# The first two branch gates as one pair of seven products, queries and keys in their place, and values ahead of the x0 projections

## The chip, the cores and the metric

The kernel runs on one core of one Trainium2 chip. A core has TensorE (PE, matrix products into the accumulators of PSUM), VectorE (DVE), ScalarE (ACT), GpSimd (POOL) and SyncE (SP, which here does nothing but issue DMAs). The metric is the device time of one execution in microseconds (us); lower is better.

## The reference, cut to what matters

One layer of a hybrid backbone is computed for 128 context tokens and 512 latent tokens, 640 in all, with 1,024 channels in float32. The layer input is modulated (`h = x * (1 + scale) + shift`) and goes through one wide projection; everything else hangs on it:

```python
z = h @ w_in
hy, g_h, qkv, g_a, m = split(z)
v_h, x1, x0 = split(short_conv(hy))             # Hyena branch
q, k, v = split(qkv)                            # attention branch, 16 heads of 64
y_h = (fft_conv(v_h * x1, filters) + d * v_h * x1) * x0
y_a = attention(q, k, v)                        # context, or neighbourhood plus cached context
p_h = (y_h * silu(g_h)) @ w_bh
p_a = (y_a * silu(g_a)) @ w_ba
out = (sigmoid(m_h) * p_h + sigmoid(m_a) * p_a) @ w_out
y = layer_norm(alpha * x + gate * out)
```

The branch gates of the title are tiles of `g_a`; values are `v`; the x0 projections give `x0`. The keys and values of the context tokens are outputs too (`new_k`, `new_v`).

## The kernel before, in words

**Precision and tiles.** Channels lie on the 128 partitions, tokens along the free dimension. The modulated input is kept as a high and a low part (`hH`, `hL`, split by `split`, L101), eight blocks of 128 channels each; blocks 2 and 3 lie in tiles of their own (`hHp`, `hLp`). A weight tile is 1,024 input channels by 128 output channels and is split likewise into `wh` and `wl`. A product is three matmuls: high by high, high by low, low by high. A projection tile (`proj`, L188; `accumulate`, L178) is 8 blocks x 3 products x 2 halves of 320 tokens, into two of the four accumulator banks of `ps_mm`. With "dma" a weight's low part is made by a ScalarE negation (L162), an accumulating GpSimd DMA (L163) and a ScalarE copy for the high part (L164), with no VectorE work. There are two `raw`, two `wh` and three `wl` buffers.

**Pairs by seven products.** In the heads two weight tiles are computed together as a 2 x 2 block product (two halves of tokens, two tiles) with seven block products in place of eight (`pair_tile`, L1213). A block product is 4 blocks x 3 products, in matmuls of 320 tokens. Its operands are sums of token blocks, `t1` to `t4`, made in the first stage by `token_sums` and kept in DRAM (`tok_d`), and sums of weight blocks (`blocks`, `sum1`, `sum6`). The order of the products and of the operands they take is

```python
ORDER = ("b11", "t2", "t3", "t1", "b21", "t4", "b22")
```

`high` (ScalarE, L1191) and `low` (VectorE, L1199) make the weight parts four products ahead, and `post` combines the products on VectorE (L1221, L1226).

**First stage.** After a prologue (modulation, first tiles), a planner orders the instructions by their place in the program and by the times it expects. The program there is a weave of a main line and a side line, two steps of the first to three of the second. The main line runs over rounds q: `quarter_head(q + 1)` (two v_h and two x1 tiles, each with a short convolution on VectorE, L490), `quarter_tail(q)` (two x0 tiles, with convolutions too), and in the first two rounds `values(2 + q)`, which stores its result to DRAM; then `hand_over` with the last x0 tiles, values(1) and values(0), the first queries and keys, and the weights of the first two gate tiles. A convolution needs one of two `zs` buffers, into which ScalarE empties the accumulators (L482 to L486), and `u` or `x1` buffers (four and two of them). Values need two accumulator banks and, for the fifth block of tokens, a third; those stored to DRAM are copied through the two buffers that x1 also uses. The side line computes the filter spectra (L379 on) and the long convolution (L540 on) by matmuls and VectorE products.

**Heads.** From `first_gates` on, the order on all engines is written out by hand (`manual_schedule`), SyncE's DMAs included. First come the two gate tiles, with the first three weight parts of pair 0 between them; then `sums_of_second` (two accumulating loads for pair 1), `scratch` (four copies that put `hHp` and `hLp` into the second half of token rows 0 and 1 of `hH` and `hL`, and hand the freed tiles over as scratch), the loads of t1, of pair 1's block, of t4, and the first biases. `keys` (L856) loads the cached keys, and `k_half` stores the context keys with

```python
nc.sync.dma_start(o["new_kT"][j], kp)
```

A DMA on SyncE's queue waits there for what it reads; the DMAs behind it wait too. For each of eight heads `mains` (L1377) yields the steps of the pairs named in `HEADS`, and `attend` (L1112) gives the attention steps, which in head 0 come after fixed steps of the main line. The last stage, with the branch projections, output projection and layer norm, follows.

Of the kernel before, what the change touches and what calls it, by code (L numbers as in the profile page):

```python
# [10 lines left out]
F32 = mybir.dt.float32  # L11
# [9 lines left out]
NT = 640  # L21
# [11 lines left out]
T_Q, T_K, T_V, T_GA, T_MH, T_MA, T_BH, T_BA, T_WO = 32, 40, 48, 56, 64, 72, 80, 88, 96  # L33
# [13 lines left out]
def tile_hyena_natten_step(ctx: ExitStack, tc: tile.TileContext, a, o):  # L47
    nc = tc.nc
    P = 128
# [59 lines left out]
    out = {"x0": {}}  # L109
# [34 lines left out]
    early, raws, banks = {}, {}, {}  # L144

    def wraw(i):
        raws[i] = wp.tile([P, 1024], F32, tag="raw", name=f"raw{i}")
        load_to(raws[i][:], a["wall"][i])

    def wtile(i, eng=None, dst=None, width=P):  # L150
        if i in early:
            return early.pop(i)
        if i not in raws:
            wraw(i)
        if dst is None:
            wh = wp.tile([P, 1024], F32R, tag="wh", name=f"wh{i}")
            wl = wp.tile([P, 1024], F32R, tag="wl", bufs=3, name=f"wl{i}")
            dst = [wh[:]], [wl[:]]
        raw, n = raws.pop(i), 1024 // len(dst[0])
        if eng == "dma":  # L160
            (wh,), (wl,) = dst
            nc.scalar.activation(wl, raw[:], AF.Copy, scale=-1.0)  # L162
            nc.gpsimd.dma_start(wl, a["wall"][i], accum_op=ALU.add)  # L163
            nc.scalar.activation(wh, raw[:], AF.Copy)  # L164
        else:
            for j, (wh, wl) in enumerate(zip(*dst)):
                split(wh, wl, raw[:, n * j : n * j + n], eng)
        return [[w[c // n][:, c % n : c % n + width] for c in range(0, 1024, width)] for w in dst]
# [328 lines left out]
    def gate_tile(i, dst, eng=None):  # L497
        ps = yield from proj(i, eng=eng)
        for p, cs in zip(ps, CS):
            nc.scalar.activation(dst[:, cs], p[:, :HALF], AF.Tanh, scale=0.5)  # L500
            gate(dst[:, cs], p)

    def quarter_head(q):
        us = []
        out[f"u{q}"] = us
        for i in range(2):
            n = 2 * q + i
            u = hw.tile([P, NG + 1], F32, tag="u", bufs=4, name=f"u{n}")
            x1 = hwa.tile([P, NG + 1], F32, tag="cv", bufs=2, name=f"x1_{n}")
            yield from conv_tile(n, u)  # L510
            yield
            yield from conv_tile(8 + n, x1)
            nc.vector.tensor_tensor(u[:, :NG], u[:, :NG], x1[:, :NG], op=ALU.mult)
            us.append(u)
            yield
        out[f"whole{q}"] = True
# [10 lines left out]
    def quarter_tail(q):  # L527
        for i in range(2):
            n = 2 * q + i
            out["x0"][n] = row(yhp, "yh", f"x0_{n}", n=NG + 1)  # L530
            yield from conv_tile(16 + n, out["x0"][n])
            yield
        if q < 3:
            gate_convs(q)
# [121 lines left out]
    def values(m, home=None):  # L656
        w = [wtile(T_V + 2 * m + i, "dma", width=256) for i in range(2)]
        ps = [acc(f"v{m}_{i}") for i in range(2)]

        def passes(k):  # L660
            wh, wl = w[k // 4][0][k % 4], w[k // 4][1][k % 4]
            return ((hH, wh, k == 0, False), (hL, wh, False, False), (hH, wl, False, k == NK - 1))

        for half in range(2):
            ks = range(4 * half, 4 * half + 4)
            for k in ks:
                for x, wk, first, last in passes(k):
                    for t in range(4):
                        nc.tensor.matmul(  # L669
                            ps[t // 2][:, t % 2 * 256 : t % 2 * 256 + 256], x[:, k, P * t : P * t + P], wk,  # L670
                            start=first and t % 2 == 0, stop=last, skip_group_check=True,
                        )
                yield
            if half:
                parts = [ps[0][:], ps[1][:]]
            else:
                pe = acc(f"ve{m}")
            for k in ks:
                for x, wk, first, last in passes(k):
                    nc.tensor.matmul(pe[:, :256], x[:, k, P * 4 :], wk, start=first, stop=last, skip_group_check=True)  # L680
            yield
        if home is None:
            v = out[f"v{m}"] = slot(m, "v", f"v{m}")
            for c, p in ((0, parts[0]), (512, parts[1]), (1024, pe[:, :256])):
                nc.scalar.activation(v[:, c : c + p.shape[-1]], p, AF.Copy)
        else:
            for i, p in enumerate(parts):
                v = hwa.tile([P, NG + 1], F32, tag="cv", bufs=2, name=f"v{m}_{i}")
                nc.scalar.activation(v[:, :512], p, AF.Copy)
                nc.scalar.activation(v[:, 512:640], pe[:, 128 * i : 128 * i + 128], AF.Copy)  # L690
                nc.sync.dma_start(home[m][:, 512 * i : 512 * i + 512], v[:, :512])
                nc.sync.dma_start(home[m][:, 1024 + 128 * i : 1152 + 128 * i], v[:, 512:640])
                if i == 0:
                    nc.sync.dma_start(o["new_v"][:, m * 256 : m * 256 + 256], v[:, :256])
            yield
            return
        nc.sync.dma_start(o["new_v"][:, m * 256 : m * 256 + 256], v[:, :256])
        yield
# [61 lines left out]
    def chain(*gens):  # L760
        for g in gens:
            yield from g
# [58 lines left out]
    def queries(j):  # L821
        for hf, p in enumerate((yield from proj(T_Q + j, eng="dma"))):
            q_half(j, hf, p[:, :HALF])
        yield
# [31 lines left out]
    def keys(j):  # L856
        cached_keys(j)
        for hf, p in enumerate((yield from proj(T_K + j, eng="dma"))):
            k_half(j, hf, p[:, :HALF])
        yield  # L860

    def hand_over():
        yield from quarter_tail(3)
        load_sums(0, SUMS[:2])
        yield from values(1, v_d)
        hwa_stack.close()
        out["slots_l"] = left.enter_context(tc.tile_pool(name="slots_l", bufs=1, reuse_waits="tile"))
        out["slots_q"] = left.enter_context(tc.tile_pool(name="slots_q", bufs=1, reuse_waits="tile"))
        first_blocks()
        gate_convs(3)  # L870
        yield from chain(values(0), queries(0), keys(0))
        for i in range(2):
            wraw(T_GA + i)
        for i in range(2):
            early[T_GA + i] = wtile(T_GA + i, "dma")
        load_a(0)

    def first_gates():
        yield from gate_a(0)
        for g in range(AHEAD - 1):  # L880
            if g == 1:
                sum1(0)
            high(g)
            low(g)
        yield from gate_a(1)

    tail = ctx.enter_context(ExitStack())
    ac = ctx.enter_context(ExitStack())
# [26 lines left out]
    at = sp = tp = None  # L915
# [203 lines left out]

    N_ATT = 4  # L1120

    def gate_a(j):
        out[f"sg{j}"] = sg = at.tile([P, NT], F32, tag="sg", bufs=2, name=f"sg{j}")
        yield from gate_tile(T_GA + j, sg[:], "dma")
        yield


    def operand(name, p):
        if name in tok:
            return lambda i, k: tok[name][i][k // 2][:, HALF * (k % 2) : HALF * (k % 2) + HALF]  # L1130
# [173 lines left out]
        return pair_tile(p, use)  # L1304

    N_PAIR = 14
    HEADS = ("q1 h0 m0", "q2 h1 m1", "q3 m2 a2", "q4 h2 m3", "q5 m4 a4", "q6 h3 m5", "q7 a6", "m6 m7")
    MAKE = dict(a=gates_a, h=gates_h, q=queries_keys, m=mix)

    def tiles_of(item):  # L1310
# [12 lines left out]

    def quarters():
        for q in range(3):
            yield from chain(quarter_head(q + 1), quarter_tail(q))
            if q < 2:
                yield from values(2 + q, v_d)

    def convs():  # L1330
        yield from chain(until("whole0"), long_conv(0))
# [65 lines left out]

    engines = {getattr(mybir.EngineType, e) for e in ("PE", "DVE", "Activation", "Pool", "SP")}
    with tc.manual_schedule(engines=engines):
        for _ in first_gates():  # L1400
            pass
        sums_of_second()
        scratch()
        load_sums(0, SUMS[2:3])
        load_sums(1, SUMS[2:3])
        load_a(1)
        load_sums(0, SUMS[3:])
        load_sums(1, SUMS[3:])
        biases[0] = [bias_tile(h) for h in range(2)]
        for j in range(8):  # L1410
            side, n_main, n_side = attend(j), N_PAIR * len(HEADS[j].split()), N_ATT if j < 7 else N_ATT + 3
            done = taken = 0
            for _ in mains(j):
                done += 1
                while done in (14, 24, 36) if j == 0 else taken * n_main < done * n_side:
                    if next(side, StopIteration) is StopIteration:
                        break
                    taken += 1
                    if j == 0:
                        break  # L1420
            for _ in side:
                drain()
        drain()
# [311 lines left out]
```

## Time and profile before

| | us |
|---|---|
| median of 3 runs | 883.93 (883.04 to 885.12) |
| the profiled execution | 883.7 |
| its span, first to last instruction | 881.9 |
| TensorE busy | 866.0 (98%) |
| VectorE busy | 645.1 (73%) |
| ScalarE busy | 450.2 (51%) |
| GpSimd busy | 189.0 (21%) |

All times within the execution are counted from the start of the span. Stages: the prologue lasts to about 50 us, the first stage with the planner to about 344, the two gate tiles to 358, the heads to about 703, and the branch and output projections to the end. Matmuls are pipelined: the record of one is longer than the time to the next, so rates are read from counts in a stretch. "Granted clock" is the share of TensorE's full clock.

### The profile page before, as it was taken

The numbers are of one execution on the slowest core, as the hardware profiler recorded it, in microseconds if no ns is written. First come the engines' busy times: TensorE is split into PE (matmuls) and PEld (weight loads), VectorE is DVE, ScalarE is ACT, GpSimd is POOL, SyncE is SP. The second block draws the span as 40 slices with busy tenths as digits, with TensorE's granted clock in tenths as the row PEclk, the third lists the DMA queues.
The fourth block names the chain that finished last, engine by engine and source line by source line (L and its number), as shares of the span: only waits on it lengthen the run. The fifth ranks groups of instructions, "written<-read, shape, count | busy, mean of one in ns | idle before, by whom it ended". The sixth has DMA issues, their size and how long they took to land.

```text
span 881.9 us, 17167 instructions
## 1 busy us (share of the span) xinstructions
PE 866.0 (98%) x6464; PEld 836.8 (95%) x6464; DVE 645.1 (73%) x1229; ACT 450.2 (51%) x960; POOL 189.0 (21%) x216
## 2 busy tenths in 40 slices
PE   8999999989999999999999999999999999999996
PEld 7899999979999999999999999999999999999885
DVE  4778986596895852787867787677778488667666
ACT  4396555546446453566566556656666532243200
POOL 0012210100100112084353334333454200000000
PEclk9999999989999999999999999999999999999999
DMA  8978886435664799978776668675854587445521
GB/s 326 400 170 226 231 215 145 92 103 138 162 132 96 202 228 241 308 218 252 172 238 164 220 153 260 138 212 158 232 138 120 180 301 246 160 165 187 183 88 56
DMA packets 75822, 168.82 MB, mean 191 GB/s; under 512 B 11067, under 2 KB 29243, under 8 KB 75740
## 3 DMA queue, kind: packets, MB, share of 16 engines
q1 hardware_dynamic: 56492, 123.32, 41.9%
q0 software_dynamic: 13632, 38.80, 22.8%
q10 hardware_dynamic: 5616, 5.61, 1.9%
q8 instruction: 51, 0.84, 0.4%
q14 instruction: 31, 0.25, 0.1%
HBM read 143.06 MB, written 23.99 MB: 189 GB/s over the span
## 4 chain that ended last, share of the span: by engine, by line
PE 94%; DVE 3%; DMA 1%; ACT 1%; issue 1%; SPq 0%; POOL 0%; POOLq 0%; DVEq 0%; ACTq 0%
PE mm L183 33%; PE sp L1238 30%; PE out L1545 6%; PE v L669 5%; PE s L1044 2%; PE s L951 2%; PE pt L1035 2%; PE ve L680 1%; DMA t<-tok_d 1%; PE adaT L253 1%; PE adaT L270 1%; PE yb L171 1%; PE yb L173 1%; PE yb L172 1%; PE ut L547 1%
## 5 line engine op out<-in xcount | busy, mean ns | idle before, releaser
L1238 PE MATMUL sp<-t,wb 128*128 128x320 f32 x1056 | 166.3, 311 | 0.4 <-DMA t<-tok_d 0.4
L1238 PEld LDWEIGHTS sp<-t,wb 128*128 128x128 f32 x1056 | 157.1, 188 | 1.2 <-DMA t<-tok_d 0.6
L1238 PE MATMUL sp<-hH,wb 128*128 128x320 f32 x524 | 126.4, 312 | 0.0
L1238 PEld LDWEIGHTS sp<-hH,wb 128*128 128x128 f32 x524 | 90.0, 188 | 2.6 <-issue 2.6
L163 POOL DMA_DIRECT2D wl<-wall x32 | 28.4, 889 | 248.2 <-ACT wl L162 212.5
L1238 PE MATMUL sp<-hL,wb 128*128 128x320 f32 x262 | 81.0, 309 | 0.0
L183 PE MATMUL mm<-hH,wh 128*128 128x320 f32 x312 | 77.6, 315 | 0.9 <-ACT hH L329 0.6
L183 PE MATMUL mm<-hH,wl 128*128 128x320 f32 x312 | 75.0, 312 | 0.4 <-DVE wl L103 0.4
L183 PE MATMUL mm<-hL,wh 128*128 128x320 f32 x312 | 74.7, 311 | 0.0
L1199 DVE TENSOR_TENSOR wb<-s,wb 128x512 fp32r<-128x512 f32 x66 | 47.1, 715 | 23.3 <-ACT wb L1191 23.2
L164 ACT ACTIVATE wh<-raw 128x1024 fp32r<-128x1024 f32 x32 | 34.0, 1061 | 58.9 <-PE mm L183 49.5
L1191 ACT ACTIVATE wb<-s 128x512 fp32r<-128x512 f32 x66 | 41.6, 632 | 37.8 <-PE sp L1238 19.1
L1006 POOL TENSOR_SCALAR edge<-edge,sm 128x320 f32<-128x320 f32 x32 | 43.1, 1526 | 66.6 <-DVE sm L1004 66.6
L183 PEld LDWEIGHTS mm<-hH,wh 128*128 128x128 f32 x312 | 53.6, 190 | 2.9 <-ACT zs L485 0.9
L1006 POOL TENSOR_SCALAR p<-p,sm 128x384 f32<-128x384 f32 x32 | 50.9, 1675 | 25.3 <-PE sp L1238 11.4
L183 PEld LDWEIGHTS mm<-hH,wl 128*128 128x128 f32 x312 | 53.1, 189 | 1.2 <-DVE wl L103 0.9
L183 PEld LDWEIGHTS mm<-hL,wh 128*128 128x128 f32 x312 | 53.1, 189 | 0.7 <-DVE hL L330 0.5
L1238 PEld LDWEIGHTS sp<-hL,wb 128*128 128x128 f32 x262 | 49.3, 188 | 0.0
L1545 PE MATMUL out<-woh,yhs 128*128 128x512 f32 (+1 forms) x176 | 45.5, 372 | 0.0
L1226 DVE TENSOR_TENSOR spare_hHp<-sp,yu 128x320 f32<-128x320 f32 x66 | 32.0, 484 | 17.3 <-PE sp L1238 11.8
L183 PE MATMUL mm<-yhs,wh 128*128 128x320 f32 x224 | 42.5, 309 | 0.0
L102 ACT ACTIVATE wh<-raw 128x1024 fp32r<-128x1024 f32 x15 | 15.8, 1058 | 46.9 <-PE mm L183 38.7
(414 smaller groups left out, 2269.1 us busy)
## 6 DMA issues: line engine op xcount, KB each, us to landing
raw<-wall SPq DMA_DIRECT2D x52, 512.0 KB, 3.8
wl<-wall POOLq DMA_DIRECT2D x32, 512.0 KB, 6.7
ra<-wall SPq DMA_DIRECT2D x22, 512.0 KB, 4.2
rb<-wall SPq DMA_DIRECT2D x42, 256.0 KB, 5.1
ada<-wada SPq DMA_DIRECT2D x16, 512.0 KB, 8.2
tm<-bias SPq DMA_DIRECT2D x16, 512.0 KB, 8.6
s<-wall SPq DMA_DIRECT2D x22, 256.0 KB, 4.5
s<-wall POOLq DMA_DIRECT2D x22, 256.0 KB, 4.4
```

The costliest lines, as they stand in the source:

```text
L163: nc.gpsimd.dma_start(wl, a["wall"][i], accum_op=ALU.add)
L164: nc.scalar.activation(wh, raw[:], AF.Copy)
L183: nc.tensor.matmul(ps[hf][:, :HALF], wt[k], x[:, hf * HALF : (hf + 1) * HALF], start=(i == 0 and k == 0), stop=(i == lead[2] and k == NK - ...
L669: nc.tensor.matmul(ps[t // 2][:, t % 2 * 256 : t % 2 * 256 + 256], x[:, k, P * t : P * t + P], wk, start=first and t % 2 == 0, stop=last, ...
L951: nc.tensor.matmul(dst[h], x[rows(h), qs], y[rows(h), ks], start=i == 0, stop=i == 2, skip_group_check=True)
L1006: nc.gpsimd.tensor_scalar_mul(pv, pv, sm[:, 2, c : c + 1])
L1035: nc.tensor.transpose(pt[:, i * P : i * P + P], ps[h][:, c : c + P], ident)
L1191: nc.scalar.activation(made[g][:, 0], block(g), AF.Copy)
L1199: nc.vector.tensor_tensor(made[g][:, 1], block(g), f(made[g][:, 0]), op=ALU.subtract)
L1226: nc.vector.tensor_tensor(c, dst, c if j == 3 else ps["u"], op=ALU.add)
L1238: nc.tensor.matmul(dst, wk, x(xi, k), start=j < 4 and k == 0 and i == 0, stop=k == 3 and i == 2, skip_group_check=True,)
L1545: ins = nc.tensor.matmul(dst, m[k][:, c0 : c0 + P], w[:, c : c + n], start=(first and k == 0), stop=(last and k == 5), skip_group_check=True,)
```

## The change

Tiles 0 and 1 of the branch gates are no longer two single tiles ahead of the heads, but one more pair, `a0`, second in head 0. `first_gates` becomes `first_head`: the first queries and the first keys are computed where the gate tiles were, with the same three weight parts of pair 0 between them; `hand_over` ends after values(0) with the two weight tiles of queries and keys. The attention steps of head 0 come at main steps 14, 32 and 48 of 56 instead of 14, 24 and 36 of 42. In the rounds of the first stage the values are placed before the x0 projections (`quarter_tail`) instead of after them.

```diff
     gate_convs(3)
-    yield from chain(values(0), queries(0), keys(0))
-    for i in range(2):
-        wraw(T_GA + i)
-    for i in range(2):
-        early[T_GA + i] = wtile(T_GA + i, "dma")
+    yield from values(0)
+    for t in (T_Q, T_K):
+        wraw(t)
+    for t in (T_Q, T_K):
+        early[t] = wtile(t, "dma")
     load_a(0)
 
-def first_gates():
-    yield from gate_a(0)
+def first_head():
+    yield from queries(0)
     for g in range(AHEAD - 1):
         if g == 1:
             sum1(0)
         high(g)
         low(g)
-    yield from gate_a(1)
+    yield from keys(0)
...
-def gate_a(j):
-    out[f"sg{j}"] = sg = at.tile([P, NT], F32, tag="sg", bufs=2, name=f"sg{j}")
-    yield from gate_tile(T_GA + j, sg[:], "dma")
-    yield
...
-HEADS = ("q1 h0 m0", "q2 h1 m1", "q3 m2 a2", "q4 h2 m3", "q5 m4 a4", "q6 h3 m5", "q7 a6", "m6 m7")
+HEADS = ("q1 a0 h0 m0", "q2 h1 m1", "q3 m2 a2", "q4 h2 m3", "q5 m4 a4", "q6 h3 m5", "q7 a6", "m6 m7")
...
 def quarters():
     for q in range(3):
-        yield from chain(quarter_head(q + 1), quarter_tail(q))
+        yield from quarter_head(q + 1)
         if q < 2:
             yield from values(2 + q, v_d)
+        yield from quarter_tail(q)
...
-    for _ in first_gates():
+    for _ in first_head():
         pass
...
-            while done in (14, 24, 36) if j == 0 else taken * n_main < done * n_side:
+            while done in (14, 32, 48) if j == 0 else taken * n_main < done * n_side:
```

## The prediction

> **What bounds the kernel now.** I read the page first, then busy time by stretch, then the timelines of the two places where TensorE loses time, then SyncE's queue.
>
> ```profile
> span 881.9 us, 17167 instructions
> PE 866.0 (98%) x6464; PEld 836.8 (95%) x6464; DVE 645.1 (73%) x1229; ACT 450.2 (51%) x960; POOL 189.0 (21%) x216
> PEclk9999999989999999999999999999999999999999
> ```
>
> TensorE is busy for 98% of the span, so a gain is either fewer matmuls or less lost time, and what another engine gains counts only there. The columns of the next rows are the stretch, its length, each engine's busy time and count, the granted clock, DMA share and GB/s.
>
> ```profile
> 171.00:178.00 7.00, 7.00 (x49) 6.92 (x48) 7.00 (x12) 3.80 (x6) 1.43 (x2) 1.00 0.82 199
> 178.00:186.00 8.00, 3.71 (x17) 2.43 (x16) 8.00 (x8) 3.99 (x8) 1.47 (x2) 0.77 0.72 176
> 186.00:189.00 3.00, 3.00 (x12) 3.00 (x13) 3.00 (x5) 1.54 (x3) 0.00 (x0) 0.50 0.28 71
> 189.00:196.00 7.00, 7.00 (x51) 6.91 (x50) 7.00 (x12) 1.46 (x6) 0.00 (x0) 0.99 0.08 21
> 740.00:760.00 20.00, 20.00 (x138) 20.00 (x138) 14.75 (x17) 4.06 (x6) 0.00 (x0) 1.00 0.62 215
> ```
>
> The last row is undisturbed projection: 20.00 / 138 = 0.145 us for a matmul of 320 columns, in issue rate (the 0.31 us of a single record overlaps its neighbours). The first four show the one large loss of the first stage. Before and after it, 100 matmuls in 14 us are 7.14 a us; from 178 to 189 there are 29 in 11 us, where 78.6 would fit. That is 49.6 / 7.14 = 6.9 us lost, the part at clock 0.50 included. What TensorE waits for there:
>
> ```profile
> 180.22 0.39 PE L172 MATMUL fa<-sl,dftH 128*128 128x256 f32 x1 [0.99 <-DVE sl L103]
> 184.22 0.58 PE L171 MATMUL fb<-sh,dftH 128*128 128x256 f32 x1 [3.15 <-ACT sh L102]
> 185.80 0.63 PE L183 MATMUL mm<-hH,wh 128*128 128x320 f32 x1 [0.15 <-ACT zs L485]
> 180.03 2.87 DVE L591 TENSOR_TENSOR X<-X,F 128x2560 f32<-128x2560 f32 x1
> 184.16 0.93 DVE L490 SCALAR_TENSOR_TENSOR u<-zs,pack,u 128x641 f32<-128x641 f32 x1
> 185.19 0.28 ACT L482 ACTIVATE zs<-mm 128x128 f32<-128x128 f32 x1 [1.02 <-DVE u L490]
> ```
>
> The filter's matmuls (fa, fb) wait behind VectorE's spectral product and two convolutions. The next projection cannot fill the hole: its accumulators are held by an earlier projection until ScalarE empties them into zs at 185.19, and zs itself is released by VectorE's `u` at 184.16 + 0.93. By the program's order the tile at 171 to 178 is an x0 projection, and the one held up at 185.80 is the second.
>
> The other place is the first pair of the heads, from 358.49. These rows are TensorE's, ScalarE's and SyncE's:
>
> ```profile
> 358.49 0.31 PE L1238 MATMUL sp<-hH,wb 128*128 128x320 f32 x1
> 367.30 1.27 PE L1238 MATMUL sp<-t,wb 128*128 128x320 f32 x7
> 368.99 1.00 PE L1238 MATMUL sp<-t,wb 128*128 128x320 f32 x5 [0.41 <-DMA t<-tok_d]
> 345.34 0.54 ACT L839 ACTIVATE k<-mm 128x64 fp32r<-128x64 f32 x3
> 345.76 0.29 ACT L842 ACTIVATE kp<-mm 128x128 f32<-128x128 f32 x1
> 358.54 0.77 ACT L500 ACTIVATE sg<-mm 128x320 f32<-128x320 f32 x2 [1.91 <-PE mm L183]
> 346.07 0.34 SPq L843 DMA_DIRECT2D new_kT<-kp  x1
> 352.52 1.34 SPq L64 DMA_DIRECT2D hH<-hHp  x2
> 354.23 1.11 SPq L64 DMA_DIRECT2D hL<-hLp  x2
> 355.45 1.97 SPq L64 DMA_DIRECT2D t<-tok_d  x4
> 357.46 0.43 SPq L64 DMA_DIRECT2D ra<-wall  x1
> 357.99 2.65 SPq L64 DMA_DIRECT2D t<-tok_d  x4
> SPq L64 <- PE mm L183: 6.3, 2, 6.0
> SPq L843 <- ACT kp L842: 5.3, 2, 2.8
> ```
>
> The last two are SyncE's waits (total, times, longest). The token sums t1 and t4, eight loads, stand behind the four copies of hH and hL. These copies waited 6.0 us for the last gate tile's matmuls on token rows 0 and 1, which come first in that tile, so they left 6 us before the pair. Even so t4, the operand of the pair's sixth product, is late: seven matmuls from 367.30 take 7 x 0.145 = 1.0 us, to 368.31, and the next starts at 368.99, 0.7 us late. There is no slack to give away here.
>
> **The change part by part.** *Matmuls.* Two gate tiles are 2 x 8 blocks x 3 products x 2 halves = 96 matmuls; a pair by seven products is 7 x 4 x 3 = 84 of the same 320 columns. 12 x 0.145 = 1.7 us less. The added VectorE work (seven low parts, two sums, five combinations) is costed from
>
> ```profile
> L1199 DVE TENSOR_TENSOR wb<-s,wb 128x512 fp32r<-128x512 f32 x66 | 47.1, 715 | 23.3 <-ACT wb L1191 23.2
> L1226 DVE TENSOR_TENSOR spare_hHp<-sp,yu 128x320 f32<-128x320 f32 x66 | 32.0, 484 | 17.3 <-PE sp L1238 11.8
> ```
>
> as 9 x 0.72 + 5 x 0.48 = 8.9 us, beside 84 x 0.145 = 12.2 us of TensorE. The heads already run 22 such pairs this way, so I put it at nothing; without that cover it would be up to 8.9 us. The DMAs of the pair (512 + 5 x 256 = 1,792 KB) replace 4 x 512 = 2,048 KB and move later. The new steps 14, 32, 48 only spread the same attention steps over 56 steps instead of 42: nothing.
>
> *Queries and keys in first_head.* Their 96 matmuls stay in front of the first pair, so TensorE's work there is the same in another order. But the keys bring two DMAs into SyncE's written-out order, ahead of the copies: the load of the cached keys and the store of `kp`. SyncE holds everything behind that store until ScalarE has made `kp`, which is after the last matmul of the keys. ScalarE starts to empty a finished tile at 358.54, which is the pair's start; `kp` ends 345.76 + 0.29 - 345.34 = 0.71 us after the first copy of k, so it is ready 0.8 us after the pair's start. The store takes 0.34 us to issue, then four copies at about 0.49 (1.97 / 4, the issue rate of four loads in a row) take 2.0. The first t1 load leaves 3.1 us after the pair's start. Now it leaves at 355.45, 3.0 us before it: 6.1 us later. Queued behind are both t1 and t4, the second pair's raw block and the first biases; TensorE waits for t1 and t4. If they then arrive at the present pace, the lateness grows by the whole 6.1 us. Lower end: the present pace is partly slow.
>
> ```profile
> 355.00:363.00 8.00, 8.00 (x56) 8.00 (x56) 5.56 (x11) 4.55 (x9) 0.00 (x0) 1.00 0.89 287
> 363.00:369.00 6.00, 5.59 (x39) 5.28 (x37) 4.93 (x12) 2.79 (x8) 0.00 (x0) 1.00 1.04 408
> DMA to landing us min/median/max: 3.3/7.2/9.6
> ```
>
> The last row is the landing time of the sixteen sum loads. The first lands after 3.3 us at best; the 2,752 KB (2.82 MB) behind it at 408 GB/s take 6.9, together 10.2 us, against the 13.5 from 355.45 to 368.99. That would give back 3.3, leaving 2.8. Upper end: the second pair's two accumulating loads (512 KB) now fall into the same time, 0.52 MB / 408 = 1.3 more, 7.4. I take the middle of 2.8 and 6.1, **+4.5 us**. The keys' own finishing copies also wait for the cached keys, now loaded late; I cost that at nothing because the wait for t1 covers it, and it reaches TensorE only if t1 is early.
>
> *Values in front of x0.* In the second round, where the loss sits, TensorE would have values at 171 instead of an x0 projection. Values need no zs and nothing of VectorE:
>
> ```profile
> 299.76 0.64 PE L669 MATMUL v<-wh,hHp 128*128 128x256 f32 x4
> 300.24 0.64 PE L669 MATMUL v<-wh,hLp 128*128 128x256 f32 x4
> 198.58 0.87 DVE L513 TENSOR_TENSOR u<-u,x 128x641 f32<-128x641 f32 x1
> ```
>
> Four matmuls take 0.48 us, so the 96 that need only two accumulators take 11.5 us, where the x0 tile took 48 x 0.145 = 7.0: 4.5 us more filling than before, against 0.99 + 3.15 + 0.15 = 4.3 us of idle time. With the idle time the halved clock behind it would go too. The x0 convolutions then fall after VectorE's crowded stretch. Against it: the values' copies go into the two buffers of x1, of which the second is released only by the product at 198.58, so accumulators may stay held. The planner also rearranges this stage. The price is between a gain of 6.9 us (all of it) and a loss of 4.3 (one more such hole); I take **-5.5**, near the gain's end, because the filler is longer than the hole, and leave 1.4 for the held buffers. The first round has no hole and the sum takes nothing from it.
>
> *The sum*, against the profiled execution's own 883.7 us (its span is 881.9, the rest lies around it; the median shown is 883.93): 883.7 - 1.7 + 4.5 - 5.5 = **881.0 us**.
>
> **The rivals.** (a) *Slower.* The hole stays: the third accumulator is asked for before the second half of the values, so TensorE stands again until 185, and the sums come 6.1 us later. For it: TensorE takes its matmuls in one planned order, and 180.22 shows it waiting with other work planned behind. Against it: the planner mixes other tiles freely. 883.7 - 1.7 + 6.1 = 888.1. It decides once less than 4.4 us of the 6.9 disappear. (b) *They cancel.* The hole goes, but the sums come 7.4 us later: 883.7 - 1.7 - 5.5 + 7.4 = 883.9. For it: DMA share 1.04 in the row above. Against it: loads of the removed gate tiles no longer compete just before. (c) *SyncE's late start costs nothing*, if the planner or the queue gets the sums in ahead: 883.7 - 1.7 - 5.5 = 876.5. Against it: the 2.8 us that the same store holds SyncE now. (d) *The hole goes, and held value buffers open another*: 883.7 - 1.7 + 4.5 + 4.3 = 890.8. (e) *The waits for the sums halve the clock* as at 186 to 189, where 12 matmuls ran in 3 us instead of 21; 5 us of that lose about 2.5: 883.5. The sums come in several short waits, which speaks against it. Beside it, the Trainium skill ("TensorE: Matmul & The Clock Gate", Part 1) says that the clock falls to half after an idle window of about 3.4 us; by that rule only an unbroken wait would do this, and the 3.15 us wait ahead of clock 0.50 roughly agrees.
>
> **How the numbers follow.** Forecast 0.34, (a) 0.26, (b) 0.15, (c) 0.12, (d) 0.08, (e) 0.05. The forecast's own range is 879.3 (sums +2.8) to 882.6 (+6.1). The range takes in (c) at its lower end and (a) with a little more at its upper: 876.0 to 889.0, with (d) and the tails outside. About 0.2%, 1.8 us, can be told from no change, so the matmul saving alone would be at the limit. Faster: (c) and nearly all of the forecast, 0.12 + 0.32 = 0.44; same: (b), (e) and the rest of it, 0.22; slower: (a) and (d), 0.34.
>
> **What would show it.** The matmuls of the heads' products must rise by 84, those of projections fall by 96. In the timeline of the first pair, the store of `kp` must stand ahead of the hH copies, and TensorE must wait for t some 2.8 to 6 us more than now; no such wait means (c). Around 170 to 190 the values must run where an x0 tile ran, and the granted clock must stay at 1.00; a gap of over 3 us with clock 0.5 means (a), one behind the values (d). The prediction is wrong at its root if the first stage does not end earlier by about 5 us, once the moved tiles are allowed for, or if the stall at the first pair is not there.

## The result and the profile after

The changed kernel takes 885.6 us (median of 20 runs, 883.81 to 887.58) against 883.98 us (20 runs, 882.82 to 885.15) before: a ratio of 1.0021, 95% interval 1.0014 to 1.0027. It is slower by 1.6 us (1.9 by the ratio), where the forecast was 881.0. Its profiled execution took 886.28 us, with a span of 884.5.

The counts are as costed. The page of the changed kernel, first part:

```profile
span 884.5 us, 17176 instructions
PE 866.5 (98%) x6452; PEld 836.1 (95%) x6452; DVE 652.4 (74%) x1243; ACT 450.0 (51%) x964; POOL 188.9 (21%) x216
```

TensorE has 12 matmuls fewer (6452 against 6464), and yet is busy 0.5 us longer.

The hole of the first stage, in busy time by stretch (stretch, length, busy time and count of each engine, granted clock, DMA share, GB/s):

```profile
171.00:178.00 7.00, 7.00 (x58) 6.91 (x59) 7.00 (x12) 4.35 (x9) 1.43 (x2) 1.00 0.77 171
178.00:186.00 8.00, 7.50 (x59) 6.94 (x57) 8.00 (x9) 1.44 (x5) 0.56 (x1) 1.00 0.25 96
186.00:189.00 3.00, 2.88 (x23) 2.71 (x23) 3.00 (x5) 2.58 (x6) 0.00 (x0) 1.00 0.02 5
```

From 178 to 189 there are 82 matmuls where there were 29, and the clock stays at 1.00. The hole is filled. (Those of the values are shorter, 0.12 us, so the count isn't a measure of the gain.)

At the first pair it went the other way. TensorE's waits of the changed kernel (total, times, longest), and then its timeline:

```profile
PE sp L1232 <- DMA t<-tok_d: 5.4, 4, 4.6
PE mm L183 <- ACT v L689: 0.8, 1, 0.8
PE fb L171 <- ACT sh L102: 0.5, 1, 0.5
```

```profile
339.92 0.31 PE L1232 MATMUL sp<-hH,wb 128*128 128x320 f32 x1
...
350.03 0.61 PE L1232 MATMUL sp<-t,wb 128*128 128x320 f32 x1 [4.65 <-DMA t<-tok_d]
350.92 1.70 PE L1232 MATMUL sp<-t,wb 128*128 128x320 f32 x5 [0.28 <-DMA t<-tok_d]
352.93 0.63 PE L1232 MATMUL sp<-t,wb 128*128 128x320 f32 x1 [0.31 <-DMA t<-tok_d]
353.75 1.70 PE L1232 MATMUL sp<-t,wb 128*128 128x320 f32 x5 [0.18 <-DMA t<-tok_d]
...
358.19 1.92 PE L1232 MATMUL sp<-t,wb 128*128 128x320 f32 x12
```

The pair starts at 339.92 (358.49 before). Of these 18.6 us, 96 x 0.145 = 13.9 are the gate tiles that no longer stand ahead of it; the other 4.7 are the hole. One wait of 4.65 us for t1 follows, and the next six matmuls, with a short wait among them, take 2.6 us instead of 0.9. The last row is the product that uses t4. The stretches of the changed kernel:

```profile
335.00:340.00 5.00, 5.00 (x38) 5.00 (x37) 4.39 (x8) 0.48 (x2) 0.00 (x0) 1.00 0.98 356
340.00:345.00 5.00, 5.00 (x36) 5.00 (x35) 4.65 (x14) 3.90 (x12) 3.33 (x8) 1.00 0.83 249
345.00:350.00 5.00, 0.39 (x3) 0.12 (x1) 1.77 (x4) 0.00 (x0) 0.00 (x0) 0.76 1.05 285
350.00:355.00 5.00, 4.19 (x12) 3.13 (x13) 0.00 (x0) 0.00 (x0) 0.00 (x0) 0.50 0.97 339
355.00:360.00 5.00, 5.00 (x27) 5.00 (x27) 3.18 (x9) 2.79 (x8) 0.00 (x0) 0.71 1.04 414
```

From 345 to 360 there are 42 matmuls where 15 / 0.145 = 103 would fit: 61 x 0.145 = 8.9 us lost, the part at clock 0.50 and 0.71 included. The pair before lost 0.7. SyncE's timeline of the changed kernel shows the predicted order, the store of `kp` ahead of the copies:

```profile
335.14 0.97 SPq L64 DMA_DIRECT2D t<-tok_d  x2
340.73 0.34 SPq L843 DMA_DIRECT2D new_kT<-kp  x1
341.16 1.17 SPq L64 DMA_DIRECT2D hH<-hHp  x2
342.37 1.93 SPq L64 DMA_DIRECT2D hL<-hLp  x2
344.43 4.05 SPq L64 DMA_DIRECT2D t<-tok_d  x4
348.52 0.43 SPq L64 DMA_DIRECT2D ra<-wall  x1
349.05 2.59 SPq L64 DMA_DIRECT2D t<-tok_d  x4
```

SyncE issues nothing from 336.1 to 340.73. The four copies take from 341.16 to 344.43, 3.3 us (2.0 were forecast). The loads of t1 leave at 344.43, 4.5 us after the pair's start (3.1 were forecast). Before, they left 3.0 us ahead of it, so they are 7.5 us later.

### The profile page after: what moved, and what is told of

Its sections match the earlier page's. It is cut to its first block, busy times and chain, and to the rows that moved or that the text cites. A ratio compares the mean times of both kernels' runs of the same rounds, so it can differ in the third digit from the quotient of the medians.

```text
span 884.5 us, 17176 instructions
## 1 busy us (share of the span) xinstructions
PE 866.5 (98%) x6452; PEld 836.1 (95%) x6452; DVE 652.4 (74%) x1243; ACT 450.0 (51%) x964; POOL 188.9 (21%) x216
## 4 chain that ended last, share of the span: by engine, by line
PE 93%; DVE 3%; DMA 1%; ACT 1%; issue 0%; SPq 0%; POOL 0%; POOLq 0%; ACTq 0%
PE sp L1232 32%; PE mm L183 32%; PE out L1540 6%; PE v L669 4%; PE s L1044 2%; PE s L951 2%; PE pt L1035 2%; PE ve L680 1%; PE adaT L253 1%; DMA v_d<-v 1%; DMA t<-tok_d 1%; PE adaT L270 1%; PE yb L171 1%; PE yb L173 1%; PE yb L172 1%; PE ut L547 1%
## 5 line engine op out<-in xcount | busy, mean ns | idle before, releaser
L1232 PE MATMUL sp<-t,wb 128*128 128x320 f32 x1104 | 176.5, 313 | 5.4 <-DMA t<-tok_d 5.4
L1232 PEld LDWEIGHTS sp<-t,wb 128*128 128x128 f32 x1104 | 165.6, 189 | 7.3 <-issue 5.4
L1232 PE MATMUL sp<-hH,wb 128*128 128x320 f32 x548 | 132.9, 314 | 0.0
L1232 PEld LDWEIGHTS sp<-hH,wb 128*128 128x128 f32 x548 | 95.0, 190 | 2.6 <-issue 2.6
L183 PE MATMUL mm<-hH,wh 128*128 128x320 f32 x288 | 69.4, 313 | 1.5 <-ACT v L689 0.8
L183 PE MATMUL mm<-hH,wl 128*128 128x320 f32 x288 | 69.5, 311 | 0.4 <-DVE wl L103 0.4
L183 PE MATMUL mm<-hL,wh 128*128 128x320 f32 x288 | 69.7, 311 | 0.0
L164 ACT ACTIVATE wh<-raw 128x1024 fp32r<-128x1024 f32 x30 | 31.9, 1063 | 42.0 <-PE mm L183 32.5
L183 PEld LDWEIGHTS mm<-hH,wh 128*128 128x128 f32 x288 | 48.5, 188 | 3.0 <-ACT v L689 1.0
L1185 ACT ACTIVATE wb<-ra 128x512 fp32r<-128x512 f32 x46 | 29.1, 633 | 25.8 <-PE sp L1232 10.7
```

Of the source, the lines that this page charges most:

```text
L183: nc.tensor.matmul(ps[hf][:, :HALF], wt[k], x[:, hf * HALF : (hf + 1) * HALF], start=(i == 0 and k == 0), stop=(i == lead[2] and k == NK - ...
L1185: nc.scalar.activation(made[g][:, 0], block(g), AF.Copy)
L1232: nc.tensor.matmul(dst, wk, x(xi, k), start=j < 4 and k == 0 and i == 0, stop=k == 3 and i == 2, skip_group_check=True,)
```

## The experiments

The parts were taken apart first, then the loss at the first pair. Every time is a median, in five rounds beside the kernel before, with the ratio to it and its 95% interval. The kernel before had medians of 883.8 to 884.6 us in these sets. So differences are taken from the ratios, times 884 us; where the medians give another number, it stands beside it. By the intervals, a difference between two edits is good to 0.9 to 1.6 us.

**Values ahead of x0, alone.** The kernel before with this edit only:

```diff
-        yield from chain(quarter_head(q + 1), quarter_tail(q))
+        yield from quarter_head(q + 1)
         if q < 2:
             yield from values(2 + q, v_d)
+        yield from quarter_tail(q)
```

> The kernel before with nothing but the values placed in front of the x0 projections. Theory: the 6.9 us hole between 178 and 189 shrinks to about 2 us, the heads stay as they were, and the time is about 879 (884.0 - 5). Rival: the order of the first stage is only shifted and the hole of the changed kernel shrank because the side line had less to share with at its end; then 883 to 885.

Measured: 878.65 us, ratio 0.994 (0.9929 to 0.9952), 5.3 us faster than before. TensorE's waits in it have no row for t at all; the longest in the first stage are those of the changed kernel, 0.7 us for v and 0.5 us for sh. Its first pair starts at

```profile
353.91 0.31 PE L1238 MATMUL sp<-hH,wb 128*128 128x320 f32 x1
```

which is 4.6 us earlier than before (358.49). The other 0.7 us is about what the pair lost before by the late t4. So -5.5 was nearly right for this part. This kernel beats both the one before and the changed one, and nothing tried below beats it.

**The heads' part alone.** The changed kernel with the rounds' old order (the diff above, reversed).

> The changed kernel with the values behind the x0 projections again, so that only the pair and the moved queries and keys are left of the change. Theory: the hole of 6.9 us is back and the late sums stay, 884.0 - 1.7 + 8.7 = 891. Rival: the two parts are not additive, because a first stage that ends later leaves the loads more time; then 886 to 888.

Measured: 888.85 us, 1.005 (1.0037 to 1.0062): 4.4 us slower than before (4.9 against the median of 883.98), between the two expectations. With the 1.7 us of matmuls saved, the heads' part costs 6.1 us here. The two parts alone make -5.3 + 4.4 = -0.9; together they made +1.9. Filling the hole thus makes the loss at the first pair about 2.8 us larger, which neither part shows alone.

The trace of this run is of its fastest execution, 886.31 us. In it the t1 loads leave 3.8 us after the pair's start, behind the store. But the DMA engines move less than in the changed kernel while SyncE is held (126 and 188 GB/s):

```profile
344.28 0.31 PE L1232 MATMUL sp<-hH,wb 128*128 128x320 f32 x1
348.09 2.24 SPq L64 DMA_DIRECT2D t<-tok_d  x4
340.00:345.00 5.00, 5.00 (x36) 5.00 (x35) 1.39 (x3) 1.82 (x7) 0.62 (x1) 1.00 0.79 126
345.00:350.00 5.00, 4.73 (x33) 4.47 (x31) 4.91 (x14) 3.27 (x9) 0.00 (x0) 1.00 0.56 188
```

The t1 loads are 6.9 us later against the pair's start than before. (This execution lost less than the 6.1 us of the set.)

**The store on ScalarE's queue.**

```diff
-            nc.sync.dma_start(o["new_kT"][j], kp)
+            (nc.sync if j else nc.scalar).dma_start(o["new_kT"][j], kp)
```

> The changed kernel, but the store of the first kp (64 KB) is issued on ScalarE's queue, so that SyncE is not held by it. Theory: the wait for t1 and t4 in the first pair comes from that hold; the copies leave as soon as the first matmuls of the keys are done, about 6 us ahead of the pair, the first pair loses under 1 us where the changed kernel loses 9.4, and the time falls by 8 to 9 us to about 877 (ratio to the kernel before about 0.992). Rival: the sums are late because yu stores, accumulating loads and sum loads now share the DMA engines in the same few us; then the hold is not what decides, and the time stays at 884 to 886.

Measured: 888.47 us, 1.0047 (1.0034 to 1.006), slower than with the store in the way. Moving it let the planner reorder SyncE's queue: the first loads of t1 now stood ahead of the second half's t2 and t3, and waited there 3.1 us for a row that the long convolution's last product frees. SyncE's wait for it and TensorE's for the sums in this run:

```profile
SPq L64 <- DVE yu L475: 3.1, 1, 3.1
PE sp L1232 <- DMA t<-tok_d: 6.5, 5, 2.9
```

Both expectations were missed. The run says nothing on the hold, since another wait took its place.

**The same, with the order held.** The copies are also kept behind the loads of t2 and t3.

```diff
-        scratch()
+        with tc.issue_after(sums_in):
+            scratch()
```

> The changed kernel with the store of the first kp on ScalarE's queue and the four copies kept behind the loads of t2 and t3, so that SyncE's order is that of the changed kernel without the store. Theory: t1 is then held only by the rows that the long convolution's last product frees at about 340.4, 0.5 us after the pair's start, instead of leaving at 4.5 us; the wait of 4.65 us shrinks to 1 to 2 us without a halved clock, and the time falls by 6 to 8 us to 878 to 880. Rival: the sums are late by the transfers that end the first stage and by the shorter time, whatever SyncE's order; then it stays within 2 us of 885.6.

Measured: 885.95 us, 1.0018 (1.0009 to 1.0026), no faster than the changed kernel. SyncE's waits in this run (total, times, longest) show why it doesn't decide either:

```profile
SPq L64 <- DMA new_kT<-kp: 7.0, 1, 7.0
```

The second pair of copies waits 7.0 us for the store, though the store is on another engine's queue. In this run's trace the transfers issued by SyncE and ScalarE take turns on eight completion semaphores. The store and the copy that waits for it have the same one, number 105, eight places apart. The hold had only changed its form.

**A hold alone, in the kernel before.** A 64 KB store of the second gate tile on SyncE, in front of the four copies:

```diff
+        nc.sync.dma_start(hold_d[:], out["sg1"][:, :P])
```

> The kernel before with one thing added: behind the second gate tile SyncE gets a store of 64 KB of that tile, which it can issue only when VectorE has made it, about 1 us after the first pair has begun. It stands in front of the four copies, as the store of kp does in the changed kernel. Theory: the hold alone delays t1 and t4 and gives a wait of about 5 us at t1 and a lossy clock after it, 6 to 9 us in all: 890 to 893. Rival: the hold is harmless where the transfers of the long convolution's end and the accumulating loads are already over, as here; then 884 to 886.

Measured: 891.85 us, 1.0082 (1.0069 to 1.0096): 7.3 us slower (7.9 by the medians). There a hold is sufficient. The pair and its copies start at

```profile
360.29 0.31 PE L1240 MATMUL sp<-hH,wb 128*128 128x320 f32 x1
361.75 1.44 SPq L64 DMA_DIRECT2D hH<-hHp  x2
```

The copies leave 1.5 us after the pair's start, where before they left 6.0 us ahead of it: 7.4 us later, at a price of 7.3 us. The stretches of this run show what the DMA engines do meanwhile:

```profile
355.00:360.00 5.00, 5.00 (x37) 5.00 (x36) 3.44 (x6) 2.07 (x5) 0.00 (x0) 1.00 0.16 28
360.00:365.00 5.00, 5.00 (x37) 5.00 (x36) 4.02 (x8) 3.39 (x7) 0.00 (x0) 1.00 0.34 113
```

They stand nearly idle (DMA share 0.16 and 0.34). In the changed kernel the share is 0.98 and 0.83 from 335 to 345, around its hold: there the engines are working off other transfers. That suggested that taking the hold away there gains less.

**The wait filled.** 32 matmuls on old data before the fourth product of pair 0, their result unused, so that the clock isn't lowered.

```diff
+            if p == 0 and j == 3:
+                warm = aux("warm")[:, :HALF]
+                for _ in range(32):
+                    nc.tensor.matmul(warm, hH[:, 4, :P], hH[:, 4, :HALF], start=True, stop=True, skip_group_check=True)
```

> The changed kernel with 32 matmuls of 320 columns, whose result nobody reads, in front of the fourth product of the first pair, about 4.7 us of work where TensorE waits 4.65 us for t1. Theory: the wait is followed by about 7 us at a halved clock, which costs some 2.5 us by itself; with TensorE kept at work the clock stays at 1.00 and the time falls by about 2 to 2.5 us to 883. Rival: the lateness of t4 alone sets the end of the first pair, whatever the clock; then the time stays within 1 us of 885.6.

Measured: 884.84 us, 1.0008 (1.0 to 1.0017), mean granted clock 0.998 against 0.992. 32 x 0.145 = 4.6 us of useless work cost nothing, and the full clock gained about 1 us (0.8 by the medians, 1.1 by the ratios), at the edge of what the rival allows. The halved clock takes place, but most of the loss is there without it.

**The store truly out of the way.** It is issued behind the last load of t4; the copies keep their place behind t2 and t3.

```diff
-            nc.sync.dma_start(o["new_kT"][j], kp)
+            if j:
+                nc.sync.dma_start(o["new_kT"][j], kp)
+            else:
+                out["kp0"] = kp
...
         load_sums(1, SUMS[3:])
+        nc.sync.dma_start(o["new_kT"][0], out["kp0"])
```

> The changed kernel with SyncE's store of the first key tile moved behind the last load of token sums (t4), and the four copies of hH and hL kept behind the loads of t2 and t3 of the second half. In the run with that store on ScalarE's queue the second pair of copies still waited for it 7.0 us, because the hardware transfers share a ring of eight completion semaphores; here nothing of the store is ahead of the copies on any queue. Theory (the hold by the key store is the larger part of the loss at the first pair): the copies are issued by 338 us, t1 between 340.5 and 343, and lands by 346 to 348; TensorE waits for t at most 2.5 us in place of 5.4, and the time is 878 to 881 us. Rival (the transfers and the rows freed at the end of the first stage, right at the pair's start, decide whatever SyncE's order): waits of 4 us or more remain, and the time is 884 to 886.5 us.

Measured: 884.38 us, 1.0008 (0.9999 to 1.0017): 1.2 us less than the changed kernel. The time is the rival's; TensorE's waits for t are 3.8 us in all, just under its 4. Stretches of this run:

```profile
335.00:340.00 5.00, 5.00 (x38) 5.00 (x37) 4.38 (x8) 0.48 (x5) 0.39 (x1) 1.00 0.90 299
340.00:345.00 5.00, 5.00 (x35) 4.85 (x33) 4.68 (x13) 3.50 (x10) 2.94 (x8) 1.00 1.05 398
345.00:350.00 5.00, 1.68 (x7) 0.97 (x7) 0.94 (x3) 0.00 (x0) 0.00 (x0) 0.96 1.07 319
350.00:355.00 5.00, 4.55 (x17) 4.55 (x18) 2.05 (x5) 1.71 (x4) 0.00 (x0) 0.50 1.05 387
```

The DMA engines are now full from 340 on, and TensorE still stands. The transfers of 335 to 360 us, first in the changed kernel, then here (size of one, median us from issue to landing):

```profile
t<-tok_d SPq DMA_DIRECT2D x10, 320.0 KB, 5.5
```

```profile
t<-tok_d SPq DMA_DIRECT2D x10, 320.0 KB, 7.9
```

The sums are issued earlier and travel 2.4 us longer in the median.

**The copies on ScalarE.** In addition the four copies of 160 KB are made by activations instead of transfers, and t1's loads are kept behind t3's.

```diff
-                load_to(f(t[:, k, HALF:]), f(t[:, 2 + k, :HALF]))
+                nc.scalar.activation(t[:, k, HALF:], f(t[:, 2 + k, :HALF]), AF.Copy)
```

> The changed kernel with the key store late, as in the run before, and the four copies of 160 KB inside hH and hL made by ScalarE (four activations) instead of four transfers; t1's loads are kept behind t3's. In the run with the late store alone the copies landed 0.43 to 0.45 us apart, ahead of t1, with the DMA engines busy 0.9 to 1.07 from 335 to 360 us. Theory (the transfers themselves, not the order on SyncE's queue, now bound the sums): t1 and t4 land 1.8 us sooner and the time is 882.6 us (881.8 to 883.4). Rival (the rows freed by the last product, or another wait at issue, decide): 884.4 us within 0.6.

Measured: 883.16 us, 0.9989 (0.998 to 0.9998): 1.7 us less than the run before it (1.2 by the medians), and inside the range expected of the transfers. The copies also leave SyncE's queue here, so this run alone does not tell bytes from places in the queue. The next one does, because its loads stand on GpSimd's queue.

**And without the second pair's accumulating loads.**

```diff
-        sums_of_second()
```

> The same kernel as with the copies on ScalarE, and also the two accumulating loads of the second pair's block sums (256 KB each, GpSimd's queue) left out, so that this pair computes with blocks not summed. They took 1.29 and 1.66 us between the landings on either side of them, one ahead of the last t1 load and one ahead of t4. Theory (transfers bound the sums): t1's last load 3.1 us and t4 4.7 us sooner than with the late store alone, and the time is 879.7 us (878.9 to 880.6). Rival (rows freed or waits at issue): within 0.6 us of 884.4.

Measured: 879.42 us, 0.9946 (0.9933 to 0.996), as expected of the transfers. TensorE's waits and stretches of this run:

```profile
PE sp L1239 <- DMA t<-tok_d: 1.5, 2, 1.1
```

```profile
345.00:350.00 5.00, 3.86 (x24) 3.33 (x23) 1.99 (x4) 1.44 (x4) 0.00 (x0) 1.00 1.01 399
350.00:355.00 5.00, 4.61 (x38) 4.14 (x38) 3.69 (x12) 2.73 (x11) 0.00 (x0) 1.00 1.01 367
```

3.8 us came off for 512 KB of accumulating loads (3.7 by the medians), more than the 3.0 us that they take between other landings. The clock now stays at 1.00 as well; whether that is the rest of the 3.8 wasn't measured.

**The hold put back into this lighter kernel.** The store in its old place, the rest as in the last run.

> The kernel with the copies on ScalarE and without the second pair's two accumulating loads, with one thing put back: the store of the first key tile in its old place on SyncE, ahead of the loads of t1 and t4. Theory (transfers and freed rows bound the sums; the hold is worth little by itself): the store holds t1 some 1 to 2 us beyond the time at which its rows come free, and the time is 879.4 to 881 us. Rival (the hold has a price of its own of about the 4.5 us that the prediction gave it): 883 to 885 us.

Measured: 880.73 us, 0.9962 (0.9949 to 0.9974): 1.4 us more, give or take 1.6, inside the first range and not in the rival's. Here the four copies no longer stand between the store and t1. So in both kernels from which the hold was taken away, it was worth 1.2 to 1.4 us.

**Only the accumulating loads left out of the changed kernel.**

> The changed kernel with nothing else altered than that the two accumulating loads of the second pair's block sums are left out, so that this pair computes with blocks not summed; the store, the copies and their order stay. Theory (transfers add to the hold): the two loads' 3.0 us come off, 882.6 us (881.8 to 883.6). Rival (the hold alone decides when the sums land): within 0.7 us of 885.6 us.

Measured: 884.17 us, 1.0 (0.9992 to 1.0009): 1.9 us less than the changed kernel (1.4 by the medians), outside both ranges. The loads count, but by about half of what they are worth with the store and the copies gone (3.8). TensorE's longest wait is still 3.2 us:

```profile
PE sp L1232 <- DMA t<-tok_d: 4.2, 3, 3.2
```

So the causes don't add up one by one. While one of them still keeps t1 late and the clock low, taking another away gains little.

**The steps of the attention.** The changed kernel with 14, 24 and 36 again.

```diff
-                while done in (14, 32, 48) if j == 0 else taken * n_main < done * n_side:
+                while done in (14, 24, 36) if j == 0 else taken * n_main < done * n_side:
```

> The changed kernel with the attention's steps of the first head after products 14, 24 and 36, as before the change, in place of 14, 32 and 48. The prediction priced this edit at nothing: expected within 0.6 us of the changed kernel's 885.6 us. Rival (the later steps push the first head's attention into later work and cost over 1 us): below 884.6 us.

Measured: 885.48 us, 1.0019 (1.0011 to 1.0027), no difference from the changed kernel's 885.6.

## Why the prediction was wrong, point by point

**Matmuls, -1.7.** The count fell by 12, as said; no run measured the 1.7 us by themselves. The extra VectorE work and the new steps of the attention show in no wait; the steps by themselves cost nothing (885.48 against 885.6).

**Values in front of x0, -5.5.** Right in its mechanism: the values run where the x0 tile ran, the clock stays at 1.00, and the edit alone gave -5.3. The size is in part luck. 4.6 us came at the hole, and 0.7 at t4, which the term did not contain. Rivals (a) and (d) fall: the two waits left there are 0.5 us and 0.8 us, the second for ScalarE's copies of the values (the held buffers of the prediction).

**Token sums, +4.5.** This is the step that failed, as a size. Out of the ratios the term is 1.9 + 1.7 + 5.3 = 8.9 us (8.6 by the medians); by the trace 8.9 - 0.7 = 8.2. All lie above even the upper end of 7.4. With 8.2 the sum of the prediction gives 883.7 - 1.7 - 5.5 + 8.2 = 884.7, and the measured median is 885.6. Three things were wrong in it:

- *The sums were to make up time behind the hold.* The price was the middle between the full 6.1 us and 2.8, in which the sums land 10.2 us after the first t1 load leaves, instead of 13.5. In the changed kernel it is 13.8 us from that load (344.43) to the start of t4's product (358.19): nothing was made up. And the load left 7.5 us later than before, not 6.1. Of these 1.4 us, 1.3 are the four copies, priced at 0.49 us each by a row of loads; their own rows in the prediction (1.34 and 1.11 us for two) gave 0.6, and in the changed kernel it was 0.8.
- *The hold was taken for nearly the only cause.* Other transfers stood only in the upper end, at 1.3 us. A hold is enough by itself where the DMA engines have room: 7.3 us in the kernel before with a hold added (DMA share 0.16 and 0.34). The heads alone, where less is moved during the hold, lose 6.1 us; no run took the hold out of that kernel. Both are more than 4.5. But in the changed kernel the hold is not needed. With the store out of the way 1.2 us came off, and about 7.7 of the 8.9 stayed, because other transfers fill the same time (share 0.90 to 1.07 from 335 to 355). That transfers bound the sums there is shown: taking away 640 KB of copies and then 512 KB of accumulating loads, with the hold gone, brought 1.7 and 3.8 us. Against the best case of 877.0 (before, less 1.7 and 5.3) 2.4 us are still missing in that run. SyncE still waits 3.1 us in it for rows that the convolution's last product frees; whether that is what is missing stays open.
- *What the removed tiles had kept apart was not counted.* The two gate tiles were 13.9 us of TensorE work that lay between the end of the long convolution and the first pair. The last products of the convolution on VectorE, in the timelines before, after, and with the heads alone:

```profile
337.28 1.46 DVE L475 TENSOR_TENSOR yu<-x,u 128x64 f32<-128x64 f32 x4
338.95 1.44 DVE L475 TENSOR_TENSOR yu<-x,u 128x64 f32<-128x64 f32 x4
336.14 1.42 DVE L475 TENSOR_TENSOR yu<-x,u 128x64 f32<-128x64 f32 x4
```

  From the product's end to the pair's start (358.49, 339.92 and 344.28) it was 19.8 us; now the pair starts 0.5 us before it ends; with the heads alone it is 6.7 us. Rows for t1 that this product frees, its stores, the second pair's block sums and the sums of the second half all fall into the time in which t1 and t4 are due. The distance by itself is not shown to be a cause of the whole loss: the kernel before with a hold added keeps the two gate tiles there and loses 7.3 us. Of the two kernels with the hold and without the gate tiles, the one with the shorter distance loses 2.8 us more (8.9 against 6.1). No run moved the distance alone.

Rival (e) was set aside for a wrong reason: "several short waits" was the forecast, and one of 4.65 us came, with clock 0.50 in it and behind it. Of its 2.5 us the filled wait gained about 1. Rival (c) falls already with the changed kernel's order, in which the store stands ahead; the late store adds that the sums are late even without the hold. Rival (b) came nearest, at 883.9: its 7.4 is the nearest of the prices, though 0.8 to 1.5 too small. The loads that it added are shown to count, by 1.9 us in the changed kernel.

## What to carry to other kernels

Work that is taken away in front of a stage also takes away time in which that stage's transfers landed: list all transfers that are due in the time that its loads need (13.8 us here) with their bytes, not only those behind the instruction that now waits. Two causes can each be enough for a loss. Here a hold cost about its full length where the DMA engines had room (7.3 us for 7.4), and taking it away gained 1.2 us where they were working off something else; the DMA share of that stretch tells which. Where a change has two parts, time each alone before both: here one of them was worth 5.3 us, and the other gave it all back.

## What the runs showed of the hardware that was not expected

The clock fell to half without a long wait. In the run with the late store, TensorE's timeline has three waits close together:

```profile
346.47 1.00 PE L1235 MATMUL sp<-t,wb 128*128 128x320 f32 x5 [1.20 <-DMA t<-tok_d]
348.34 0.41 PE L1235 MATMUL sp<-t,wb 128*128 128x320 f32 x1 [0.87 <-DMA t<-tok_d]
350.45 1.70 PE L1235 MATMUL sp<-t,wb 128*128 128x320 f32 x5 [1.70 <-DMA t<-tok_d]
```

None is longer than 1.7 us, with six matmuls between them, and the clock from 350 to 355 is 0.50 (its stretch stands above). In the lighter kernel with the hold put back the waits at the same place are of 0.59, 0.31 and 0.91 us, and the clock stays at 1.00:

```profile
345.00:350.00 5.00, 3.44 (x19) 2.84 (x20) 0.99 (x2) 0.00 (x0) 0.00 (x0) 1.00 0.98 338
350.00:355.00 5.00, 4.16 (x25) 3.38 (x24) 3.85 (x10) 3.10 (x9) 0.00 (x0) 1.00 1.04 410
```

With the copies on ScalarE the waits in the second of these stretches are of 2.10 and 0.31 us, with 14 matmuls in it, and the clock then falls:

```profile
350.00:355.00 5.00, 2.58 (x14) 1.82 (x12) 3.84 (x10) 2.79 (x8) 0.00 (x0) 1.00 1.06 356
355.00:360.00 5.00, 4.62 (x25) 4.43 (x27) 2.64 (x9) 2.00 (x7) 0.00 (x0) 0.66 1.04 403
```

In these runs the clock fell after 7 and after 14 matmuls in 5 us, and not after 19. The Trainium skill ("TensorE: Matmul & The Clock Gate", Part 1) names an idle window of about 3.4 us. The single wait of 4.65 us is longer than that, but the clock fell about 2.2 us into it: the wait began at 345.38, and 0.76 from 345 to 350 puts the fall at 347.6. Before the change it is the same with the wait of 3.15 us that the prediction took as agreeing with this rule: it began at 181.07, and 0.77 from 178 to 186 puts the fall at 182.3. So the stretch that lowers the clock need not be without any matmul.

Also unexpected: a transfer on one engine's queue waited 7.0 us for one on another engine's, by the shared completion semaphore.
